# Summing the first adaLN half on the tensor engine, block by block, with x moved up among the first loads

## The chip, the cores and the metric

The kernel runs on one core of a Trainium2 chip. The metric is the device time of one execution in microseconds (us), the median of several runs. A core has a tensor engine (PE; its weight loads are shown apart as PEld), a vector engine (DVE), a scalar engine (ACT), GpSimd (POOL) and a sync engine (SP), which here issues the large loads. Each engine takes its instructions in a fixed order and waits at the first that isn't ready.

## The reference, cut to what matters

The model is a decoder trunk of two layers over 256 rows of width 1024. Ahead of each sub-layer the rows are normalized, then scaled and shifted by vectors that come from a conditioning vector c through a large matrix, w_ada:

```
c_act = jax.nn.silu(c)
for layer in range(DEPTH):
    mod = jnp.einsum('bd,dn->bn', c_act, w_ada[layer]) + b_ada[layer]
    sh1, sc1, gt1, sh2, sc2, gt2 = [m[:, None, :] for m in jnp.split(mod, 6, axis=-1)]
    ...
    h = rms_norm(x, g_attn[layer]) * (1.0 + sc1) + sh1
    y = hybrid_mixer(h, ...)
    x = x + gt1 * y
    ...
```

The change is to how sh1 and sc1 of layer 0 are summed, for the first 512 of the 1024 columns. A "half" below is such a set: 512 columns of the shift and the same 512 of the scale, 1024 columns of w_ada together. A "block" is 128 of the 1024 rows of w_ada for one half, a tile of 128 x 1024 float32 (512 KB). Eight blocks make a half.

## The kernel before, in words

All is written in `trunk`. Everything is laid out for 128 partitions; the 256 rows of x are two tiles t of 128 rows, the width 1024 is eight chunks k of 128. Matrix products of activations with weights are made of three products of parts (`split_w` makes the two parts of a weight tile on ACT and DVE, `split_act` those of an activation).

The start stands between lines 407 and 472, in a pool of its own and under two rules. `in_order()` chains all DVE instructions of the block in the order in which they are written, and all ACT instructions likewise. PE's and SP's orders are left to the framework, which sorts by program order and by what is ready. Loads of w_ada in the start use eight buffers (`rada`, `bufs=8`); the ninth block can be loaded once the first buffer has been read.

The order as written:

- `first` and `second` are `Start` objects for half 0 and half 1. `block(k)` issues the load of block k on SP and then, on DVE, multiplies it with column k of the activated c (`cT`, one number for each partition) and adds it to `acc`, 128 x 1024 (lines 429 to 435).
- The first loop (line 438) goes over the eight blocks of half 0. Behind blocks 1 and 5 it issues the load of a tile of x, with its sum of squares (`nm0.part`, ACT) and its normalization (`nm0.finish`, ACT, with a small DVE and a small POOL step). At block 5 it also transposes the vectors (`vrows`) on PE; DVE copies out the norm's gains gT and the biases bT.
- `pj_i.split(0, 4)` loads and splits the first unit of w_in (line 451). Then comes block 0 of half 1.
- `first.sums()` (line 420) brings half 0 onto the partitions: `acc` still holds 128 partial sums per column. One matmul with the identity opens the accumulation in PSUM with the bias; eight matmuls, with 128 columns of `acc` each as the stationary operand and one column of ones as the moving one, sum over the partitions. The result `pc` has eight columns, four of shift and four of scale. `m1.take` (line 237) copies the shift and makes the gain on DVE.
- `modulated` (line 294) transposes four chunks of the normalized x on PE and applies gain and shift, for t = 0 on ACT and for t = 1 on DVE. `split_h` makes the two parts of h. Between these stand blocks 1 and 2 of half 1 on DVE.
- PE then runs the first half of the first projection (`pj_i.unit`, 324 columns) and most of the second (`pj_a.unit`, 512 columns), while DVE works off blocks 3 to 7 of half 1. `second.sums()` and its modulation follow, and with the second half of h the projections are finished. Attention begins behind that.

Of the kernel before, what the change touches and what calls it, by code (L numbers as in the profile page):

```python
# [12 lines left out]
F32 = mybir.dt.float32  # L13
# [7 lines left out]
P = 128  # L21
# [34 lines left out]
def trunk(ctx: ExitStack, tc: tile.TileContext, x, c, positions, w_in, w_out, diff_lambda, diff_subln,  # L56
          w_ada, b_ada, g_attn, g_ffn, w_ff_gate, w_ff_up, w_ff_down, w_router,
          w_exp_gate, w_exp_up, w_exp_down, g_final, out):
    nc = tc.nc
    V, A, T, G = nc.vector, nc.scalar, nc.tensor, nc.gpsimd  # L60
# [9 lines left out]
    def ps_b(name):  # L70
        return psum.tile([P, 512], F32, tag="b", name=name, bufs=2)

    def ps_c(name):
        return psum.tile([P, 512], F32, tag="c", name=name, bufs=2)
# [8 lines left out]
    def pre1(shape, dt, name):  # L83
        return pre.tile(shape, dt, name=name, bufs=1)
# [13 lines left out]
    ident = cst.tile([P, P], F32, name="ident")  # L98
# [9 lines left out]
    cT = pre1([P, KC], F32, "cT")  # L108
# [26 lines left out]
    @contextmanager  # L135
    def in_order(engines=(V.engine, A.engine)):

        ins = nc.cur_bb.bb.instructions
        n0 = len(ins)
        yield  # L140
        last = {}
        for i in ins[n0:]:
            if i.engine in engines:
                if i.engine in last:
                    tc.add_manual_dep(i, last[i.engine], mybir.DependencyInfo(
                        mybir.DependencyClass.NoSync, mybir.DependencyReason.DATA), reason="in_order")
                last[i.engine] = i.name
# [65 lines left out]
    class Mod:  # L213


        def __init__(self, l, which, g0, queue):
            self.l, self.base, self.g0, self.queue = l, which * 3072, g0, queue
            self.piece = 3 * which
            self.sh = cst.tile([P, KC], F32, name=f"sh{l}{which}")
            self.gain = cst.tile([P, KC], F32, name=f"gain{l}{which}")  # L220
# [41 lines left out]
    m1 = Mod(0, 0, 0, nc.scalar)  # L262
# [31 lines left out]
    def modulated(xn, mod, t, q, on_act):  # L294

        pt = ps_c("pt").rearrange("p (k s) -> p k s", k=4)
        hp = wk.tile([P, 4, P], F32, tag="hp", name="hp")
        for j in range(4):
            k = 4 * q + j
            T.transpose(pt[:, j], xn[:, t, k * P:(k + 1) * P], ident)  # L300
        for j in range(4):
            modulate(on_act, hp[:, j], pt[:, j], mod, 4 * q + j)
        return hp

    def split_h(hp, t, q, h1, h2):
        ks, s = slice(4 * q, 4 * q + 4), slice(t * P, (t + 1) * P)
        split_act(h1[:, ks, s], h2[:, ks, s], hp)
# [101 lines left out]
    with tc.tile_pool(name="start", bufs=1, reuse_waits="tile") as sp, tc.issue_after(silu_c.ins), in_order():  # L409

        bT = sp.tile([P, 2, KC], F32, name="bT")

        class Start:


            def __init__(self, q):
                self.q = q
                self.acc = pre.tile([P, 1024], F32, tag="ada", name="ada", bufs=ADAB)

            def sums(self):  # L420
                q = self.q
                pc = ps_b("pc")
                T.matmul(pc[:, 0:8].rearrange("p (a k) -> p a k", a=2), ident, bT[:, :, 4 * q:4 * q + 4],
                         start=True, stop=False)
                for j in range(8):
                    T.matmul(pc[:, j:j + 1], self.acc[:, j * P:(j + 1) * P], ones[:, 0:1], start=False, stop=j == 7)
                m1.take(q, pc)

            def block(self, k):
                r = sp.tile([P, 1024], F32, tag="rada", name="rada", bufs=8)  # L430
                nc.sync.dma_start(r, w_ada[0, self.q, k])
                if k == 0:
                    V.tensor_scalar(self.acc, r, cT[:, 0:1], None, op0=ALU.mult)
                else:
                    V.scalar_tensor_tensor(self.acc, r, cT[:, k:k + 1], self.acc, op0=ALU.mult, op1=ALU.add)

        first, second = Start(0), Start(1)
        for k in range(KC):
            first.block(k)
            if k in (1, 5):  # L440
                t = k // 5
                nc.sync.dma_start(xs[:, t], x[0, t * P:(t + 1) * P, :])
                for n in range(2):
                    nm0.part(t, n)
                nm0.finish(t, True)
            if k == 5:
                pv = ps_c("pv")
                T.transpose(pv[:, 0:48], vrows, ident[:48, :48])
                V.tensor_copy(gT, pv[:, 0:32])
                V.tensor_copy(bT.rearrange("p a k -> p (a k)"), pv[:, 32:48])  # L450
        vi = pj_i.split(0, 4)
        second.block(0)
        first.sums()
        hps = [modulated(nm0.xn, m1, t, 0, t == 0) for t in range(NT)]
        for t in range(NT):
            second.block(1 + t)
            split_h(hps[t], t, 0, *h)
        pj_i.unit(0, 4, vi)
        *va, a2 = pj_a.split(0, 4, True)
        pj_a.unit(0, 4, va, terms=(0, 1))  # L460
        for k in range(3, KC):
            second.block(k)
        a2()
        *vi, i2 = pj_i.split(4, 4, True)
        second.sums()
        hps = [modulated(nm0.xn, m1, t, 1, t == 1) for t in range(NT)]
        for t in range(NT):
            split_h(hps[t], t, 1, *h)
            if t == 0:
                i2()  # L470
        pj_i.unit(4, 4, vi)
        pj_a.unit(0, 4, va, terms=(2,))
# [468 lines left out]
    with tc.tile_pool(name="ffn", bufs=1, reuse_waits="tile") as fp:  # L941
# [5 lines left out]
        m1 = Mod(1, 0, 8, nc.gpsimd)  # L947
# [585 lines left out]
```

## Time and profile before

| | us |
|---|---|
| median of 3 runs | 1309.76 (1303.88 to 1314.73) |
| profiled execution, its own time | 1308.91 |
| its span, first to last instruction | 1307.1 |
| PE busy | 1230.5 (94%) |
| DVE busy | 1091.4 (83%) |
| ACT busy | 832.9 (64%) |
| DMA | 396.90 MB, mean 304 GB/s |

The times in the rows below count from the first instruction. "Busy" of PE includes matmuls that stand in the pipeline behind one another, so a full PE is not PE at its peak. The granted clock (PEclk) is the share of the full TensorE clock of 2.4 GHz that the hardware granted; the record of it begins with its first change.

### The profile page before, as it was taken

The numbers are of one execution on the slowest core, as the hardware profiler recorded it, in microseconds if no ns is written. First come the engines' busy times: TensorE is split into PE (matmuls) and PEld (weight loads), VectorE is DVE, ScalarE is ACT, GpSimd is POOL, SyncE is SP. The second block draws the span as 40 slices with busy tenths as digits, with TensorE's granted clock in tenths as the row PEclk, the third lists the DMA queues.
The fourth block names the chain that finished last, engine by engine and source line by source line (L and its number), as shares of the span: only waits on it lengthen the run. The fifth ranks groups of instructions, "written<-read, shape, count | busy, mean of one in ns | idle before, by whom it ended". The sixth has DMA issues, their size and how long they took to land.

```text
span 1307.1 us, 17866 instructions
## 1 busy us (share of the span) xinstructions
PE 1230.5 (94%) x6601; PEld 1036.0 (79%) x6601; DVE 1091.4 (83%) x1236; ACT 832.9 (64%) x1010; POOL 52.5 (4%) x88
## 2 busy tenths in 40 slices
PE   4989899999999899899999999999999999999996
PEld 4779779989887787677888877788878778788784
DVE  7898677787768864687899987899986999978996
ACT  3654563433446555457788856788855898667785
POOL 3101000010001000000000000000000000000001
PEclk9999899999989899889999999999999999999999
DMA  9557828988963433568999998899998999998991
GB/s 382 206 170 239 293 93 309 318 315 302 331 241 113 137 122 129 225 235 290 385 396 420 419 412 308 324 404 420 421 382 292 358 419 420 420 350 319 410 361 56
DMA packets 63679, 396.90 MB, mean 304 GB/s; under 512 B 7718, under 2 KB 8032, under 8 KB 23264
## 3 DMA queue, kind: packets, MB, share of 16 engines
q1 hardware_dynamic: 62928, 395.60, 79.4%
q8 instruction: 54, 0.88, 0.3%
q14 instruction: 41, 0.34, 0.1%
q0 software_dynamic: 640, 0.07, 0.0%
q10 hardware_dynamic: 16, 0.00, 0.0%
HBM read 394.60 MB, written 1.05 MB: 303 GB/s over the span
## 4 chain that ended last, share of the span: by engine, by line
PE 62%; DVE 10%; issue 8%; ACT 4%; POOL 0%; POOLq 0%; ACTq 0%; DVEq 0%
DVE w L168 6%; PE gu L187 5%; PE gu L186 5%; PE gu L188 5%; PE gu L1269 4%; PE gu L1268 4%; PE dn L186 4%; PE dn L188 4%; PE dn L187 4%; PE pj L340 3%; PE dn L1268 3%; PE dn L1269 2%; PE ptl L1284 2%; PE gu L870 2%; PE gu L872 2%
## 5 line engine op out<-in xcount | busy, mean ns | idle before, releaser
L164 ACT ACTIVATE w<-raw 128x1024 fp32r<-128x1024 f32 (+3 forms) x203 | 258.9, 1293 | 164.4 <-PE gu L871 37.2
L168 DVE TENSOR_TENSOR w<-raw,w 128x1024 fp32r<-128x1024 f32 (+3 forms) x203 | 303.8, 1512 | 50.8 <-ACT w L164 50.3
L168 DVE TENSOR_TENSOR w<-rawx,w 128x2048 fp32r<-128x2048 f32 (+1 forms) x134 | 300.2, 2252 | 26.5 <-ACT w L164 26.2
L164 ACT ACTIVATE w<-rawx 128x2048 fp32r<-128x2048 f32 (+1 forms) x134 | 252.2, 1887 | 16.4 <-PE gu L187 9.2
L340 PE MATMUL pj<-w,h 128*128 128x384 f32 (+3 forms) x672 | 134.0, 351 | 1.2 <-ACT h L182 0.5
L211 DVE SCALAR_TENSOR_TENSOR ada<-rada,cT,ada 128x1024 f32<-128x1024 f32 x80 | 102.3, 1279 | 32.7 <-DMA rada<-in_w_ada 32.6
L340 PEld LDWEIGHTS pj<-w,h 128*128 128x128 f32 x672 | 112.9, 192 | 11.4 <-ACT h L182 2.4
L168 DVE TENSOR_TENSOR w2x<-rawx,w1x 128x2048 fp32r<-128x2048 f32 (+1 forms) x45 | 100.6, 2237 | 12.9 <-ACT w1x L164 12.9
L186 PE MATMUL gu<-w,hh 128*128 128x512 f32 (+1 forms) x288 | 110.5, 384 | 0.0
L1269 PE MATMUL gu<-w,hh 128*128 128x512 f32 (+1 forms) x288 | 107.4, 380 | 3.2 <-DVE w L168 2.8
L187 PE MATMUL gu<-w,hh 128*128 128x512 f32 (+1 forms) x288 | 109.2, 379 | 0.0
L188 PE MATMUL gu<-w,hh 128*128 128x512 f32 (+1 forms) x288 | 109.1, 379 | 0.0
L1268 PE MATMUL gu<-w,hh 128*128 128x512 f32 (+1 forms) x288 | 106.7, 377 | 0.0
L870 PE MATMUL gu<-h,w 128*128 128x256 f32 x320 | 91.5, 286 | 0.0
L872 PE MATMUL gu<-h,w 128*128 128x256 f32 x320 | 90.6, 283 | 0.0
L871 PE MATMUL gu<-h,w 128*128 128x256 f32 x320 | 90.5, 283 | 0.0
L164 ACT ACTIVATE w1x<-rawx 128x2048 fp32r<-128x2048 f32 (+1 forms) x45 | 84.4, 1878 | 4.7 <-PE gu L187 2.5
L1269 PEld LDWEIGHTS gu<-w,hh 128*128 128x128 f32 x288 | 54.1, 188 | 18.8 <-DVE w L168 8.5
L188 PEld LDWEIGHTS gu<-w,hh 128*128 128x128 f32 x288 | 54.6, 190 | 10.8
L187 PEld LDWEIGHTS gu<-w,hh 128*128 128x128 f32 x288 | 54.8, 190 | 10.4 <-issue 0.5
L186 PEld LDWEIGHTS gu<-w,hh 128*128 128x128 f32 x288 | 54.6, 190 | 10.5 <-issue 0.5
L1268 PEld LDWEIGHTS gu<-w,hh 128*128 128x128 f32 x288 | 54.1, 188 | 10.4
(348 smaller groups left out, 2508.7 us busy)
## 6 DMA issues: line engine op xcount, KB each, us to landing
rawx<-in_w_exp_down SPq DMA_DIRECT2D x72, 1024.0 KB, 7.4
rawx<-in_w_exp_up SPq DMA_DIRECT2D x55, 1024.0 KB, 7.6
rawx<-in_w_exp_gate SPq DMA_DIRECT2D x49, 1024.0 KB, 8.3
rada<-in_w_ada SPq DMA_DIRECT2D x96, 512.0 KB, 5.2
raw<-in_w_exp_gate SPq DMA_DIRECT2D x39, 1024.0 KB, 8.0
raw<-in_w_exp_up SPq DMA_DIRECT2D x33, 1024.0 KB, 7.8
raw<-in_w_exp_down SPq DMA_DIRECT2D x16, 1024.0 KB, 7.3
raw<-in_w_ff_gate SPq DMA_DIRECT2D x11, 1024.0 KB, 7.1
```

Of the source, the lines that this page charges most:

```text
L164: last_split[0] = A.activation(v1[:, s], r[:, s], AF.Copy)
L168: last_split[1] = V.tensor_tensor(v2[:, s], r[:, s], v1[:, s].bitcast(F32), op=ALU.subtract)
L186: T.matmul(ps, l1, r1, start=start, stop=False)
L187: T.matmul(ps, l2, r1, start=False, stop=False)
L188: T.matmul(ps, l1, r2, start=False, stop=stop)
L211: V.scalar_tensor_tensor(acc, r, cT[:, k:k + 1], acc, op0=ALU.mult, op1=ALU.add)
L340: T.matmul(o, (h1, h2, h1)[i][:, k, s], (v1, v1, v2)[i][:, j], start=(k == 0 and i == 0), stop=(k == KC - 1 and i == 2))
L870: T.matmul(pg[:, b], v1[:, k, s], h[0][:, k], start=(k == 0), stop=False)
L871: T.matmul(pg[:, b], v1[:, k, s], h[1][:, k], start=False, stop=False)
L872: T.matmul(pg[:, b], v2[:, k, s], h[0][:, k], start=False, stop=(k == KC - 1))
L1268: T.matmul(ps, l1, r1, start=start, stop=False)
L1269: T.matmul(ps, l1, r2, start=False, stop=stop)
```

## The change

Half 0 gets no `acc` any more. A PSUM tile `pc` is opened with a matmul of the identity with a tile of zeros. For each block, as it lands, eight matmuls take 128 columns of the block as the stationary operand and column k of cT as the moving one, and add to the eight columns of `pc`: the product with c and the sum over rows are one step. The bias matmul now closes the accumulation, and `take` follows as before. The loads of x are issued behind blocks 0 and 2 instead of 1 and 5, the transposes of the vectors at block 4 instead of 5. Half 1 stays as it was.

```diff
-        first, second = Start(0), Start(1)
+        second = Start(1)
+
+        pc = ps_b("pc")
+        zero = sp.tile([P, 8], F32, name="zero")
+        V.memset(zero, 0.0)
+        T.matmul(pc[:, 0:8], ident, zero, start=True, stop=False)
         for k in range(KC):
-            first.block(k)
-            if k in (1, 5):
-                t = k // 5
+            r = sp.tile([P, 1024], F32, tag="rada", name="rada", bufs=8)
+            nc.sync.dma_start(r, w_ada[0, 0, k])
+            for j in range(8):
+                T.matmul(pc[:, j:j + 1], r[:, j * P:(j + 1) * P], cT[:, k:k + 1], start=False, stop=False)
+            if k in (0, 2):
+                t = k // 2
                 nc.sync.dma_start(xs[:, t], x[0, t * P:(t + 1) * P, :])
                 for n in range(2):
                     nm0.part(t, n)
                 nm0.finish(t, True)
-            if k == 5:
+            if k == 4:
                 pv = ps_c("pv")
...
         vi = pj_i.split(0, 4)
         second.block(0)
-        first.sums()
+        T.matmul(pc[:, 0:8].rearrange("p (a k) -> p a k", a=2), ident, bT[:, :, 0:4], start=False, stop=True)
+        m1.take(0, pc)
```

## Rows read from the trace of the kernel before

**Rows 1.** Windows of the start: stretch, its length, busy us (instructions) by engine, PEclk, DMA share, GB/s.

```profile
5.50:17.00 11.50, 1.69 (x6) 1.07 (x6) 10.73 (x33) 4.16 (x11) 2.84 (x2) 1.00 1.03 413
...
25.90:31.10 5.20, 5.20 (x21) 5.15 (x21) 5.14 (x6) 2.35 (x3) 0.74 (x2) 1.00 1.04 411
31.10:36.20 5.10, 5.10 (x27) 4.32 (x26) 5.01 (x5) 1.38 (x2) 1.10 (x1) 1.00 1.01 412
```

**Rows 2.** Timeline of DVE in the start: start, duration, line, operation, out<-in, count.

```profile
5.89 0.96 DVE L353 CAST posf<-posi 2x128 f32<-2x128 int32 x1 [4.80 <-DMA posi<-in_positions]
...
8.77 0.74 DVE L433 TENSOR_SCALAR ada<-rada,cT 128x1024 f32<-128x1024 f32 x1
9.55 1.29 DVE L435 SCALAR_TENSOR_TENSOR ada<-rada,cT,ada 128x1024 f32<-128x1024 f32 x1
...
17.07 2.60 DVE L435 SCALAR_TENSOR_TENSOR ada<-rada,cT,ada 128x1024 f32<-128x1024 f32 x2
...
23.34 0.16 DVE L239 COPY sh<-pc 128x4 f32<-128x4 f32 x1 [1.52 <-PE pc L426]
...
28.48 6.56 DVE L435 SCALAR_TENSOR_TENSOR ada<-rada,cT,ada 128x1024 f32<-128x1024 f32 x5
```

**Rows 3.** Timeline of PE in the start.

```profile
4.84 0.27 PE L107 MATMUL pcr<-ident,crow 8*128 8x8 f32 x1 [4.84 <-POOL ident masks.py:199]
...
17.21 1.02 PE L423 MATMUL pc<-bT,ident 128*128 128x8 f32 x4 [1.70 <-DVE bT L450]
18.85 1.12 PE L300 MATMUL pt<-ident,xn 128*128 128x128 f32 x4 [0.61 <-ACT xn L284]
19.76 3.54 PE L426 MATMUL pc<-ones,ada 128*128 128x1 f32 x16
...
25.88 0.64 PE L340 MATMUL pj<-w,h 128*128 128x324 f32 x1
...
36.34 1.84 PE L426 MATMUL pc<-ones,ada 128*128 128x1 f32 x16
```

**Rows 4.** Line 426 from 19 to 24 us: durations in ns, min/median/max.

```profile
L426 PE MATMUL pc<-ones,ada x16: 340/352/352, 19.8 to 22.9; 128*128 128x1 f32 x16
```

**Rows 5.** SP's first and later w_ada issues, and each one's time to landing.

```profile
0.82 0.87 SPq L431 DMA_DIRECT2D rada<-in_w_ada  x2
DMA to landing us min/median/max: 3.5/3.5/3.5
...
4.73 1.27 SPq L431 DMA_DIRECT2D rada<-in_w_ada  x2
DMA to landing us min/median/max: 10.0/10.2/10.3
```

**Rows 6.** Windows of the projections' matmuls alone (tile pj).

```profile
26.00:31.10 5.10, 4.94 (x16) 4.38 (x17) 0.00 (x0) 0.00 (x0) 1.00 1.03 410
31.10:32.30 1.20, 1.20 (x10) 1.20 (x9) 0.00 (x0) 0.00 (x0) 1.00 1.05 432
```

**Rows 7.** Windows later on, around very narrow matmuls; columns as in rows 1.

```profile
360.90:362.20 1.30, 1.30 (x13) 1.30 (x13) 1.30 (x2) 0.28 (x1) 0.00 (x0) 1.00 0.98 403
363.20:369.00 5.80, 5.80 (x28) 5.80 (x29) 4.83 (x6) 3.18 (x4) 0.00 (x0) 0.50 0.73 238
...
543.20:546.50 3.30, 3.30 (x18) 3.17 (x17) 1.73 (x5) 2.13 (x6) 0.00 (x0) 0.50 0.68 281
546.60:549.90 3.30, 3.30 (x17) 3.08 (x17) 2.20 (x16) 2.11 (x5) 1.16 (x6) 0.50 0.01 2
550.00:553.00 3.00, 2.87 (x22) 2.25 (x22) 1.91 (x6) 2.49 (x3) 0.00 (x0) 1.00 0.00 0
```

**Rows 8.** Timeline of PE in those stretches.

```profile
360.86 2.28 PE L233 MATMUL pc<-ones,ada 128*128 128x1 f32 x16 [2.21 <-issue]
...
544.03 1.71 PE L984 MATMUL pl<-wr,hp 128*128 128x8 f32 x8
...
547.52 4.40 PE L1380 MATMUL pth<-ident,h 128*128 128x128 f32 x21
```

## The prediction

> **What bounds the kernel now.** I read the table of windows over the first 38 us first, then the timelines of PE and DVE there, then the landing of the loads, and last the granted clock wherever PE runs very narrow matmuls. In the windows the reader is to see a start that is full of DMA (its share stays above 1.0 from 5.5 to 36.2 us) while PE is nearly empty: 1.69 us busy in the 11.5 us to 17.0, against 10.73 for DVE [rows 1]. DVE spends that time on the first half's sum over w_ada: the first block's multiply of 0.74 us at 8.77, then seven multiply-adds, the last pair from 17.07 to 19.67 [rows 2]. PE then turns the sum into columns in 16 records from 19.76 to 23.30, and DVE picks the result up at 23.34 [rows 2, 3]. I call that moment T0.
>
> From T0 everything up to 38 us hangs on one thread. DVE's fixed order goes on with the seven remaining blocks of the second half, the last five from 28.48 to 35.04, 11.7 us behind T0 [rows 2]. PE starts the projection at 25.88 and is full to 36.2 [rows 1, 3]; the second half's columns start at 36.34, 13.0 us behind T0 [rows 3]. Behind this come the second half of h, the first projection's end, and attention. PE is 94% busy over the span, so I see nothing further on that would take up a shift of T0, and count it one for one.
>
> **The change part by part.** *Removed:* 0.74 + 7 x 1.29, some 9.8 us of DVE [rows 2], and the 16 records after the sum, 3.54 us [rows 3]. Both lay on the path to T0, so all of it comes free; the question is what stands there instead.
>
> *Added on PE:* for each of eight blocks 8 calls, 64 in all. A call of this form (fp32, 128x128 weights, one moving column) leaves two weight loads and two matmuls: the 8 calls of the old sum are the 16 records [rows 3]. So the change issues 128 records instead of 16. The pace of the old ones is the price: 16 took 3.54 us, one by itself lasts 0.35 [rows 4], so the spacing is (3.54 - 0.35) / 15 = 0.213 us. The same 16 at 36.34 took 1.84, about half [rows 3]. So one block costs 3.4 us at the slow pace or 1.7 at the fast one, where a 512 KB block lands every 1.3 us: the first lands at 0.82 + 3.5 = 4.3, the last of the eight, issued about 5.7, at about 16.0 (nine loads later, 11.7 us) [rows 5]. At either pace PE is the limit and not the loads.
>
> Which pace? The page shows the granted clock as 1.00 from the start, but the rows contradict that: the projection's matmuls of 324 columns run 16 in 5.1 us before 31.1 and 10 in 1.2 us after it [rows 6], a step by two, which I read as 1.2 and then 2.4 GHz. PE had been full since 25.9 by then. What raises the clock is told by the places where the record does show it. From 543.2 to 546.5 PE was busy in 3.30 of 3.30 us, mostly with matmuls of 8 moving columns, and the granted clock stayed at 0.50; eight of those records took 1.71 us, 0.214 each. It stood at 0.50 through the transposes of 128 columns from 547.52 too, and was back at 1.00 from 550 [rows 7, 8]. From 360.9 the 1-column form itself ran: busy in 1.30 of 1.30 us at 1.00, after a pause; then the clock fell in the midst of these 16 records, which is why they took 2.28 us, and it stayed at 0.50 for 5.8 us of full wide matmuls [rows 7, 8]. So, as far as these rows go, a PE that is busy with one or eight columns does not gain the full clock, and does not hold it behind a pause. The new records are all of one column, and what runs among them is eight transposes. I therefore take 0.213 throughout; the other end is half of it.
>
> The Trainium skill, "TensorE: Matmul & The Clock Gate", section "What's actually happening", says the array is throttled by default and activity releases it; read as engine busy time, that would give the fast pace soon after the start, and it is the second rival below. The stretch at 543 us speaks against that reading. The same page, section "LDWEIGHTS (loading the stationary operand)", puts a load of 128 columns at 107 ns; by that price 128 loads are 13.7 us instead of 27.3, and the end would come out at 1308.8. The trace does not agree at the lower clock: 0.213 from load to load.
>
> *The sum to T0.* PE is free of the transpose of c at 4.84 + 0.27 = 5.1 [rows 3]. The zero matmul that opens the accumulation is two records like those of the bT matmul (four in 1.02 us, 0.255 each [rows 3]): 0.5. The blocks: 128 x 0.213 = 27.3. PE must also run the eight transposes of xn (four in 1.12 us [rows 3], so 2.2), the two small ones of positions and vectors (at most 0.28 each, 0.6), and both bT matmuls (four records, 1.0). Together 5.1 + 0.5 + 27.3 + 2.2 + 0.6 + 1.0 = 36.7, and 0.1 to the pickup: T0 = 36.8 instead of 23.3, later by 13.5 us. Nothing of it is hidden: DVE, in its written order, has only the first weight unit's subtraction and the second half's first multiply before it waits for T0.
>
> *Moved:* x is issued behind blocks 0 and 2 instead of 1 and 5, so the first half of x lands one load (1.3 us) earlier and the second three. I cost this at nothing: the rows normalized last were transposed from 18.85 [rows 3], before T0 as it is, and the new T0 is later still. The order of loads changes nothing in their number.
>
> *The new wait on SP:* the second half's blocks need the eight buffers of the first, and PE now frees these, the last about T0. Behind them in SP's order stand the later units of w_in. Block 15 then lands 3.5 to 10.3 us after issue [rows 5], 40.3 to 47.1; DVE wants it about 10.5 us after T0 (the last of the five from 28.48, 33.8 before), 47.3. So this wait is covered, by little at the worst end; if it isn't, a us or two is added.
>
> *After T0* the chain of 13.0 us is as it was: PE comes to the projection at the lower clock in both kernels.
>
> The profiled execution took 1308.9 us (span 1307.1 and 1.8 around it), 0.9 under the median of the three runs shown. 1308.9 + 13.5 = 1322.4.
>
> **The rivals.**
>
> *Late order.* The zero memset could stand on DVE behind the cast that waits for positions until 5.89 and lasts 0.96 [rows 2], or where DVE had its first block before, at 8.77; PE would start at 6.9 to 8.8. Or PE meets a transpose before its xn is there. That adds 1.8 to 5: 1324 to 1327. For it: DVE's order at that place was not by arrival before either (block 0 had landed at 4.3). An upper bound on the pitch itself is 0.35, a record with no overlap: 128 x 0.14 = 17.8 more, 1340; the same form ran at 0.213, so I give this next to nothing.
>
> *The clock rises while the blocks are summed.* Suppose it takes 5.2 us of a busy PE, as from 25.9 to 31.1. Then 24 records go at 0.213 to 10.8, 104 at 0.107 to 21.9, and the rest (3.8) at half, 1.9: T0 = 23.8, half a us late. The projection then starts at the full clock and saves 2.6 us of 5.2, so that DVE's 11.7 us behind T0 is the last instead of 13.0, 1.3 less. In sum 0.8 less: about 1308.1. For it: PE would be busy without a gap. Against it: the stretches at 363 and 543 us.
>
> *The other side: faster.* If the fast pace held from the first block (the page's 1.00), the 31.6 us of PE work would be 15.8: T0 = 21.0, 2.3 earlier, and with the 1.3 of the projection 3.6: 1305.3. It decides where the mean pitch falls under 18.2 / 31.6 x 0.213 = 0.123 us, at which T0 is 23.3 as before. Against it: the old sum's own 16 records, at the same place in the program, ran at 0.213.
>
> **How the numbers follow.** Forecast 0.72, late order 0.11, rising clock 0.11, fast from the start 0.05, something else 0.01. The forecast's own range is 1319 to 1325 (an order of PE without gaps and one with short ones, and when the clock rises in the projection). The range of 8 in 10 goes from 1308, which takes in the rising clock, to 1328, which takes in the late order. Over 1%, about what a measurement of this kernel tells from no change, is 13.1 us: the forecast's 13.5 stands on that line, so its 0.72 splits, 0.37 slower and 0.35 within. Late order is slower (0.11). Rising and fast clock lie within 1% (0.16, of which I give 0.02 to faster, for scatter). Slower 0.48, same 0.50, faster 0.02.
>
> **What the profile after would show.** Right: 128 records of the new line between 5 and 37 us, 16 in about 3.4 us, with PE full; no multiply-add on DVE before the second half; the copy of the shift at about 36.8 and the second one 15 us later; loads of w_ada that wait on PE; DMA share well under 1.0 between 18 and 36. Wrong, if the same 16 records speed up on the way, or if the first projection starts before 30 us. Then the step that failed is the pace at which one-column matmuls run, and with it the reading of the clock. If T0 is at 37 and the time is not 10 us longer, the step that failed is that nothing behind it takes up the shift.

## The result, and the profile after

| | before | after |
|---|---|---|
| median, us (6 runs each) | 1310.88 | 1326.62 |
| ratio, 95% interval | | 1.013 (1.0099 to 1.0161) |
| span of the profiled execution, us | 1307.1 | 1321.5 |
| T0, the copy of the first half's shift | 23.34 | 38.56 |
| the same copy for the second half | 38.23 | 52.55 |

The kernel became slower by 1.0 to 1.6%. The profiled execution after is longer by 14.4 us; T0 came 15.2 us later and the second half's copy 14.3 us. So in these two executions the whole loss is there before the first projection is finished. DVE in the kernel after from T0 on, and the second copy of the kernel before (start, duration, line, operation, out<-in, count, and in brackets the wait before it):

```profile
38.56 0.16 DVE L239 COPY sh<-pc 128x4 f32<-128x4 f32 x1 [17.66 <-PE pc L461]
...
43.70 6.56 DVE L435 SCALAR_TENSOR_TENSOR ada<-rada,cT,ada 128x1024 f32<-128x1024 f32 x5
...
52.55 0.16 DVE L239 COPY sh<-pc 128x4 f32<-128x4 f32 x1
```

```profile
38.23 0.16 DVE L239 COPY sh<-pc 128x4 f32<-128x4 f32 x1 [0.91 <-PE pc L426]
```

All kernels named in the rows below are read from their own profiled execution.

PE in the start of the kernel after, in order of time (start, duration, line, out<-in, count):

```profile
6.92 0.26 PE L355 MATMUL pp<-ident,posf 2*128 2x2 f32 x1 [1.80 <-DVE posf L353]
7.12 0.60 PE L442 MATMUL pc<-zero,ident 128*128 128x8 f32 x2
8.57 0.31 PE L456 MATMUL pv<-ident,vrows 48*128 48x48 f32 x1 [0.85 <-DVE ang L374]
8.81 17.22 PE L447 MATMUL pc<-cT,rada 128*128 128x1 f32 x80
25.89 0.88 PE L300 MATMUL pt<-ident,xn 128*128 128x128 f32 x3
26.57 3.41 PE L447 MATMUL pc<-cT,rada 128*128 128x1 f32 x16
...
34.67 3.41 PE L447 MATMUL pc<-cT,rada 128*128 128x1 f32 x16
37.95 0.57 PE L461 MATMUL pc<-bT,ident 128*128 128x8 f32 x2
...
42.52 8.09 PE L340 MATMUL pj<-w,h 128*128 128x324 f32 x38
...
50.67 1.84 PE L426 MATMUL pc<-ones,ada 128*128 128x1 f32 x16
```

This answers [rows 3]: in place of 16 records from 19.76 to 23.30 there are 128, from 8.81 to 38.1, with the eight transposes of xn among them. Sixteen of them, one block, take 3.41 us. The same in sum, by line, from 5 to 39 us (count, busy us, mean ns of one, idle before):

```profile
L447 PEld LDWEIGHTS pc<-cT,rada 128*128 128x128 f32 x128 | 27.7, 333 | 0.1
L447 PE MATMUL pc<-cT,rada 128*128 128x1 f32 x128 | 27.6, 350 | 0.0
```

The weight loads are full for 27.7 us with 0.1 us of idle time: between these records PE waits for nothing, and the loads of w_ada land sooner than PE can take them. The windows of the kernel after, columns as in [rows 1] (the 1.00 under PEclk is no measurement here, since it stands ahead of the first recorded change of the clock), and its longest waits in the first 56 us (who waited for whom, us in total, times, longest):

```profile
5.50:17.00 11.50, 9.22 (x43) 9.05 (x43) 4.32 (x27) 5.19 (x12) 4.36 (x6) 1.00 1.02 412
17.00:38.00 21.00, 21.00 (x102) 21.00 (x101) 2.24 (x3) 1.38 (x2) 0.00 (x0) 1.00 0.64 226
```

```profile
ACT hp L290 <- DVE gain L240: 27.8, 2, 19.6
POOL kTI L530 <- PE pc L461: 22.2, 1, 22.2
DVE sh L239 <- PE pc L461: 17.7, 1, 17.7
```

From 17 to 38 us PE is busy in 21.00 of 21.00 us, DVE in 2.24 and ACT in 1.38, and the DMA share, 1.01 to 1.04 in the rows of the kernel before [rows 1], is 0.64. DVE waits 17.7 us for the sum in one piece, and ACT 19.6 for the gain. The engines have changed places: DVE was the full one, now it is PE, and PE needs longer.

### The profile page after: what moved, and what is told of

Read it like the earlier page. It is cut to its first block, busy times and chain, and to the rows that moved or that the text cites. A ratio compares the mean times of both kernels' runs of the same rounds, so it can differ in the third digit from the quotient of the medians.

```text
span 1321.5 us, 18081 instructions
## 1 busy us (share of the span) xinstructions
PE 1254.2 (95%) x6715; PEld 1059.9 (80%) x6715; DVE 1082.4 (82%) x1229; ACT 832.7 (63%) x1010; POOL 50.5 (4%) x88
## 3 DMA queue, kind: packets, MB, share of 16 engines
HBM read 394.60 MB, written 1.05 MB: 299 GB/s over the span
## 4 chain that ended last, share of the span: by engine, by line
PE 59%; DVE 12%; issue 9%; ACT 4%; POOL 0%; POOLq 0%; DVEq 0%; ACTq 0%
DVE w L168 7%; PE gu L187 5%; PE gu L186 5%; PE gu L188 5%; PE dn L186 4%; PE dn L188 4%; PE dn L187 4%; PE gu L1278 3%; PE gu L1277 3%; PE pj L340 3%; PE gu L879 2%; PE gu L881 2%; PE gu L880 2%; ACT w L164 2%; PE dn L1277 2%
```

## The experiments

Ratios are to the kernel before, run on the same chip in the same session. In the first session its median was 1306.06 us, in the second 1307.29, in the third 1307.61. Results of the kernels' wide matmuls that are told of below are thrown away; nothing of the computation is left out.

### The moved part alone

```diff
-            if k in (1, 5):
-                t = k // 5
+            if k in (0, 2):
+                t = k // 2
...
-            if k == 5:
+            if k == 4:
```

> The kernel before with only the moved part of the change: x issued behind blocks 0 and 2, the vectors transposed at block 4, the sum still on DVE. Theory (the whole loss comes from the tensor engine's 128 narrow records): the moved part is worth nothing, T0 (the copy of the shift) stays at 23.3 within 1 us, the time within 2 us of before. Rival (the moved loads themselves cost, because the blocks land later): T0 later by one or two loads, 1.3 to 2.6 us, and the time by as much.

Measured: 1307.53 us, ratio 1.0004 (0.9972 to 1.0036). T0 at 23.91, second copy at 37.80. The moved part alone changes the time by no more than 0.4% either way, so the loss belongs to the sum. (T0 is 0.6 us later. The trace shows no wait of DVE in that stretch: its multiply-adds start at 10.93 instead of 9.55, behind small steps that stood among the blocks before, and the last one ends at 20.2 instead of 19.7. Which of the steps costs this was not tested.)

### Another order on PE

Line numbers apart, the kernel after, with the rope tables (and with them the positions' transpose) moved behind block 4, and PE's transpose of the vectors ordered behind that block:

```diff
+    def tables():
         posf = pre1([NT, P], F32, "posf")
...
             if k == 4:
-                pv = ps_c("pv")
-                T.transpose(pv[:, 0:48], vrows, ident[:48, :48])
+                with tc.issue_after(mm.ins):
+                    pv = ps_c("pv")
+                    T.transpose(pv[:, 0:48], vrows, ident[:48, :48])
...
+                    tables()
```

> The kernel after with another order on the tensor engine: the rope tables and the transpose of the vectors stand behind block 4, so the blocks can start once c is activated. Theory (of the 15.2 us by which T0 came later, 3.2 are the wait of the first block behind the positions and the vectors, the rest is 128 records at 0.213): first block at 5.6 instead of 8.8, T0 at 35.3, the time 3 us under the kernel after. Rival (the loss is the pace alone and the early records wait for loads instead): first block earlier, but T0 at 37 or later and the time less than 1.5 us under after.

Measured: 1320.32 us, ratio 1.0094 (1.0063 to 1.0126). PE in its start:

```profile
5.05 0.59 PE L446 MATMUL pc<-zero,ident 128*128 128x8 f32 x2
5.50 17.20 PE L451 MATMUL pc<-cT,rada 128*128 128x1 f32 x80
...
32.10 3.41 PE L451 MATMUL pc<-cT,rada 128*128 128x1 f32 x16
35.37 0.57 PE L467 MATMUL pc<-bT,ident 128*128 128x8 f32 x2
```

The first block starts at 5.50 instead of 8.81, T0 comes at 35.99 instead of 38.56 (2.6 earlier), the second copy at 50.21 instead of 52.55 (2.3). The ratio is 0.0036 lower than that of the kernel after, 4.7 us, but the two were measured in different sessions and their intervals overlap (1.0099 to 1.0126), so the times alone don't tell them apart; the traces do. Some 2.5 us of the loss are PE's order: the first block stood behind two transposes that waited for late inputs. Of the 3.3 us by which it came earlier 2.6 are left at T0, less than expected. The other 12.7 us to T0 remain with the blocks started right behind the activation of c; they are PE's work at this pace.

### 64 moving columns instead of one

The zero tile and the matmul that opens `pc` grow to 512 columns with it.

```diff
-                T.matmul(pc[:, j:j + 1], r[:, j * P:(j + 1) * P], cT[:, k:k + 1], start=False, stop=False)
+                T.matmul(pj64[:, j], r[:, j * P:(j + 1) * P], cT[:, k:k + 1].to_broadcast([P, 64]), start=False, stop=False)
```

> The kernel after with one size changed: each of the 64 calls has 64 moving columns (column k of c repeated) instead of 1, the same weight loads, the same number of records. Theory (the tensor engine stays at 1.2 GHz because its matmuls are of one column): with 64 columns the same records speed up from 0.213 to about 0.11 to 0.12 us on the way, T0 at about 27 us, the first projection at the full clock from its start, and the time 9 to 13 us under the kernel after. Rival 1 (busy time decides, and the one-column stream was slow for another reason, such as waiting for loads or two weight loads a call): the pace stays at 0.213, T0 at 38 to 39, the time as after. Rival 2 (wider is dearer): pace over 0.213, slower than after.

Measured: 1323.97 us, ratio 1.011 (1.0038 to 1.0182). The theory fell, in the form that it had:

```profile
8.97 17.17 PE L448 MATMUL pc<-cT,rada 128*128 128x64 f32 x80
26.07 0.34 PE L457 MATMUL pv<-ident,vrows 48*128 48x48 f32 x1
26.34 10.50 PE L448 MATMUL pc<-cT,rada 128*128 128x64 f32 x48
```

80 records in 17.17 us are 0.215 each, as with one column (17.22), and the last 48 are no faster than the first. T0 is 37.21, earlier than in the kernel after because PE ran the eight transposes of xn behind the blocks and not among them. Two things follow. The columns are free at this size: 64 cost what one costs, so the pace is that of the weight loads, or of a fixed cost for each load and matmul; the runs don't part these two. And it isn't the single column that keeps the pace low; a stream of fp32 weight loads with 64 columns each stays at it just as well, through 28 us of a full PE.

### Wide matmuls ahead of the blocks, and among them

Whether 0.213 us is the clock at all was still open: it could have been the path of the weights. 24 matmuls of 512 bf16 columns were put between the zero matmul and the first block:

```diff
+        wb = sp.tile([P, 512], BF16, name="wb")
+        V.memset(wb, 0.5)
...
+                    after = T.matmul(pj_a.ps[0], wb[:, :P], wb, start=True, stop=True).ins
...
+            with tc.issue_after(last):
                 for j in range(8):
```

and in the second kernel, besides, a pair of them ahead of every second call within the blocks (8 for 16 records).

> The kernel after, with 24 wide matmuls (bf16, 512 columns, their result is thrown away) between the zero matmul and the first block; the blocks stay as they are, one column a call. With 64 columns a call the pace did not change (0.214 us), so the theory now reads: a stream that consists mostly of fp32 weight loads does not count as activity, with 1 or 64 columns, and only wide matmuls raise the clock. Theory: the burst of some 8 to 10 us raises the granted clock near its end; the first blocks then run at about 0.11 us a record and fall back to 0.213 some us later; T0 at about 41 to 44. Rival (a busy engine holds a clock that it has): all 128 records at 0.11, T0 at 29 to 32. Second rival (0.213 is not the clock but the path of the weights from freshly landed tiles): 0.213 from the first record on although the granted clock shows 1.00.

> The same burst, and 8 of the wide matmuls within each block besides, one pair ahead of every second call. Theory (wide matmuls among them keep the clock): the granted clock rises and stays at 1.00 to the end of the blocks, 16 records and 8 wide matmuls take about 3.5 us a block at that clock, T0 at 42 to 45. Rival (the narrow stream pulls the clock down even so): 6.8 us a block, T0 at 65 or later.

Measured, one run each: 1322.82 and 1327.14 us; T0 39.75 and 40.33, both earlier than expected, since the burst took 6.84 us and not 8 to 10. Windows of the records of `pc` alone (busy of PE, PEld, DVE, then PEclk, DMA share, GB/s), first with the burst alone, then with wide matmuls among them:

```profile
14.30:17.40 3.10, 3.10 (x30) 3.10 (x29) 0.00 (x0) 1.00 1.06 381
17.50:20.60 3.10, 3.10 (x17) 3.10 (x16) 0.00 (x0) 0.50 0.71 213
20.60:23.70 3.10, 3.10 (x16) 3.10 (x16) 0.00 (x0) 0.50 0.61 168
```

```profile
14.80:17.90 3.10, 1.95 (x16) 2.35 (x16) 0.00 (x0) 1.00 1.06 433
...
35.00:38.10 3.10, 1.93 (x17) 2.33 (x18) 0.00 (x0) 1.00 0.97 338
```

With the burst alone the same loads run at 29 in 3.1 us (0.107 each) while the granted clock is 1.00, and at 16 in 3.1 us (0.194 by this count, 3.41 us for 16 later) once it is 0.50. The fall comes between 17.4 and 17.5 us, 3.2 us into the narrow stream, with PE busy in every one of those windows: being busy in the profile's sense did not hold the clock that PE had. With wide matmuls among the records the clock stays at 1.00 to the end, and four records take 0.50 us throughout. So the pace is the clock, and what kept it up here were the wide matmuls. As a remedy it is worth nothing: the wide ones cost PE the time that the clock saves, T0 is no earlier.

### Two blocks on PE, six on DVE

PE opens the accumulation and takes blocks 0 and 1 directly while it is idle (NPE is 2); DVE sums the other six, and the 16 records add their sum. First with x at blocks 0 and 2, then with x at 1 and 5 as in the kernel before:

```diff
-            first.block(k)
+            if k < NPE:
+                first.direct(k)
+            else:
+                first.block(k, k == NPE)
```

> A mixture: the tensor engine takes blocks 0 and 1 directly (32 records, 6.8 us, while it is idle anyway), DVE sums blocks 2 to 7 as before, x early as in the kernel after. Theory (the direct sum costs only what does not fit into the idle time of the tensor engine): the direct records end by 16, DVE ends 1.3 us behind the landing of block 7, at 17.3 to 18.5, the 16 records follow at the slow pace, T0 at 21 to 22 and the time 1 to 2.5 us under the kernel before. Rival (the tensor engine's narrow work delays the transposes or the bias ahead of the sum): T0 at 23.3 or later and the time not under before.

> The mixture of two blocks on the tensor engine and six on DVE, now with x at blocks 1 and 5 as in the kernel before. In the mixture with x early DVE sat idle for 2.5 us behind the first of its blocks, because the step that follows x in its written order waited for ACT. Theory: without that wait DVE ends its blocks at 17.1 to 17.5, T0 at 21 and the second copy of the shift some 2 us earlier than before, the time 1.5 to 2.5 us under the kernel before. Rival (what follows T0 is held by the second half's loads or by the projection at the lower clock): T0 at 21 but the second copy at 37.5 or later, no gain.

Measured: with x early 1306.62 us, ratio 1.0000 (0.9965 to 1.0035), T0 at 24.04; with x as before 1305.79 us, ratio 0.9985 (0.9965 to 1.0005), T0 at 21.59, second copy at 35.84. DVE with x early, then with x as before:

```profile
10.41 0.74 DVE L454 TENSOR_SCALAR ada<-rada,cT 128x1024 f32<-128x1024 f32 x1
13.63 0.21 DVE L278 TENSOR_SCALAR var<-ss 128x1 f32<-128x1 f32 x1 [2.48 <-ACT xn L272]
...
16.45 3.92 DVE L456 SCALAR_TENSOR_TENSOR ada<-rada,cT,ada 128x1024 f32<-128x1024 f32 x3
```

```profile
11.18 3.92 DVE L456 SCALAR_TENSOR_TENSOR ada<-rada,cT,ada 128x1024 f32<-128x1024 f32 x3
15.02 0.21 DVE L278 TENSOR_SCALAR var<-ss 128x1 f32<-128x1 f32 x1
...
15.32 2.60 DVE L456 SCALAR_TENSOR_TENSOR ada<-rada,cT,ada 128x1024 f32<-128x1024 f32 x2
```

With x early the step after x waits 2.48 us for ACT, with blocks 3 to 7 behind it in the written order, and that eats what two blocks less on DVE had gained; the forecast of T0 at 21 to 22 missed that. With x as before nothing waits, DVE ends at 17.9 instead of 19.7, and T0 and the second copy come 1.8 and 2.4 us earlier. The median is 1.5 us under that of before, within the interval of no change.

The same with four blocks on PE:

> The mixture with x at blocks 1 and 5, now with four blocks on the tensor engine and four on DVE. Theory (each further block costs the tensor engine 16 records at 0.213, 3.4 us, and what doesn't fit ahead of DVE's end is added to T0): the direct records end at about 22.2, transposes and bias follow, then the 16 records; T0 at 28 to 29.5, against 21.6 with two blocks. Rival (the loads or DVE set T0): T0 under 24.

Measured: T0 28.56, second copy 42.45; 1306.04 us in a single run, which tells nothing beside a scatter of several us.

```profile
8.95 13.81 PE L431 MATMUL pc<-cT,rada 128*128 128x1 f32 x64
...
25.11 3.41 PE L438 MATMUL pc<-ones,ada 128*128 128x1 f32 x16
```

Two more blocks put T0 7.0 us later, 3.5 each. For two blocks PE has the idle time; the two further ones were paid in full.

### Wide matmuls in the kernel before

The kernel before has 16 records of the same form and the first projection at the low clock. 26 wide matmuls behind the transpose of the vectors and 7 behind the records, then 36 and 8:

> The kernel before, with 26 wide matmuls whose result is thrown away on the idle tensor engine ahead of the 16 records, and 7 behind them. Theory (what limits the records and the first projection is the clock at 1.2 GHz): the granted clock is up before 19.7, the 16 records take 1.8 instead of 3.5 us, T0 at 21.6, the projection of 324 columns runs at the full clock from its start (saves 2.6 us), the second copy of the shift 3 us earlier than before, the time 2 to 4 us under the kernel before. Rival (the pauses around the records bring the clock down again): T0 at 21.6 to 23.3, the projection as slow as before, gain under 1.5 us. Second rival (the wide matmuls delay the transposes): T0 later than 23.3.

> As the kernel before with wide matmuls on the idle tensor engine, now 36 ahead of the 16 records instead of 26 and 8 behind them. With 26 the granted clock had risen at 11.9 us and fallen again at 18.8, in the pauses ahead of the records. Theory (without those pauses the clock holds): granted clock 1.00 from about 12 us on, the 16 records in 1.84 us, T0 at 21.6, the first projection at the full clock, the second copy of the shift at 34 to 35.5 instead of 38.2, the time 3 to 4 us under the kernel before. Rival (the clock falls all the same, or 36 wide matmuls are too late for the sum): T0 at 23.3 or later, second copy at 37 or later, gain under 2 us.

Measured: 1303.53 us, ratio 0.9973 (0.9951 to 0.9995), and 1305.47 us, ratio 0.9973 (0.9948 to 0.9998). T0 at 23.35 and 22.64, second copy at 37.53 and 36.53. The first in windows, columns as in [rows 1], the second as PE's timeline:

```profile
12.00:18.70 6.70, 5.03 (x27) 2.62 (x25) 6.59 (x13) 3.42 (x6) 1.73 (x2) 1.00 1.02 412
18.80:23.00 4.20, 4.14 (x20) 3.98 (x21) 3.03 (x4) 1.28 (x3) 0.00 (x0) 0.50 1.03 417
```

```profile
8.99 10.71 PE L445 MATMUL pj<-wb 128*128 128x512 bf16 x36
...
20.76 1.84 PE L426 MATMUL pc<-ones,ada 128*128 128x1 f32 x16
...
34.40 1.95 PE L426 MATMUL pc<-ones,ada 128*128 128x1 f32 x16 [1.02 <-DVE ada L436]
```

With 26 the clock was up (from about 12 us on a wide matmul's record lasts 0.38 us, before that 0.63) and fell before the records came, behind pauses of PE; T0 did not move. With 36 it held: the 16 records take 1.84 us instead of 3.54. But by the same sign the clock rose only at about 15 us here, not at 12 as expected, so the last wide matmul ends at 19.7 with eight transposes still to come. The records start 1.1 us after DVE has ended, and T0 gains 0.7. The projection then runs at the full clock, and PE idles 1.02 us for DVE: behind T0 the limit is now DVE's order, 11.8 us from T0 to the end of its last block. The 2.7 to 4.2 us expected at the second copy became 1.7.

These two are under the kernel before by 0.3% with intervals that end just below 1. In the first of the two the start accounts for 0.7 us of a median 3.8 lower; the rest of that I can't assign.

### How the start passes through

| kernel | T0 | second copy | span | span less second copy |
|---|---|---|---|---|
| before | 23.34 | 38.23 | 1307.1 | 1268.9 |
| after | 38.56 | 52.55 | 1321.5 | 1269.0 |
| x moved alone | 23.91 | 37.80 | 1307.5 | 1269.7 |
| other order | 35.99 | 50.21 | 1316.3 | 1266.1 |
| 64 columns | 37.21 | 52.63 | 1323.6 | 1271.0 |
| two blocks, x as before | 21.59 | 35.84 | 1301.2 | 1265.4 |
| two blocks, x early | 24.04 | 37.93 | 1299.9 | 1262.0 |
| four blocks | 28.56 | 42.45 | 1304.3 | 1261.9 |
| 26 wide ahead | 23.35 | 37.53 | 1296.1 | 1258.6 |
| 36 wide ahead | 22.64 | 36.53 | 1304.6 | 1268.1 |
| burst, then the blocks | 39.75 | 55.26 | 1321.0 | 1265.7 |
| wide among the blocks | 40.33 | 56.24 | 1325.4 | 1269.2 |

These are single profiled executions. What follows the second copy takes 1258.6 to 1271.0 us; it scatters by several us, more than the small edits move, but it is not shorter where the start is late (1265.7 to 1271.0 in the five kernels with the second copy behind 50 us). So none of these traces shows the delay taken up behind the start; a part of it as small as the scatter could not be seen.

## Why the prediction came out as it did

The forecast was 1322.4 us, slower by 13.5; measured was a ratio of 1.0099 to 1.0161, which on the profiled 1308.9 is 13.0 to 21.1 us, and 14.4 between the two profiled executions. Direction and cause were as forecast. The median after, 1326.62, lies above the forecast's own range of 1319 to 1325, inside the wider one, and in the 1324 to 1327 of the rival called late order, which is also what the trace shows. Part of that distance is the base: the six runs of the kernel before have their median 2 us above the 1308.9 that the sum starts from. By its steps:

- *Removed.* Right: DVE's blocks and the 16 records are gone, and DVE has 2.24 us of work in the 21 us to 38.
- *128 records at 0.213, 27.3 us.* Right: 128, 27.7 us busy, 3.41 for a block, and PE rather than the loads the limit.
- *When PE starts.* This term was mis-sized. The sum let PE go on at 5.1, with the zero matmul, and booked the two small transposes as 0.6 us of work. They were waits: PE's order has the positions' transpose at 6.92, behind an input that is late, and the vectors' at 8.57, and the first block at 8.81 instead of 5.6. That is the rival called late order, with another culprit than the one named (the zero memset ran at 1.05). Undoing it was worth 2.6 us at T0. By the sum the first block was due at 6.2 with those two counted, so 2.6 late; the eight transposes and the bT matmuls, priced at 3.2 with each group's last drain in it, took 0.9 less. Hence T0 at 38.56 instead of the forecast 36.8.
- *After T0, 13.0 us as before.* It was 12.1 to the second half's records (50.67), since the clock rose sooner in the projection: its 38 matmuls took 8.09 us instead of 8.99. This took 0.9 us back, and with the term above the forecast of the shift, 13.5, comes to 14.3 at the second copy. That the two are so close is in part luck. The start was missed by 2.6 us, and two smaller misses of 0.9 went the other way, the second of them by chance: the same 38 matmuls took 7.99 us in the kernel with x moved alone and 8.98 in that with the burst.
- *The wait of SP on PE, at nothing.* It is there: SP waited 22.6 us in seven waits for PE to free buffers. It was covered, as forecast; DVE's last five blocks run without a gap from 43.70.

```profile
SPq L431 <- PE pc L447: 22.6, 7, 3.8
```

- *x earlier, at nothing.* Right for the time (1.0004), though with DVE on the path it costs 0.6 us at T0, which the forecast did not see.
- *What raises the clock.* The conclusion held, that the records stay at the lower clock; the reason given for it was too narrow. The rows [rows 7, 8] were read as "one or eight columns". 64 columns did no better. The burst and the mixed stream show what the rows of before could not: a PE that is full of such records loses a clock that it had been granted, and wide matmuls among them keep it. The rival of the rising clock is thereby excluded here, by 28 us of full PE in two kernels without a rise.

The Trainium skill, "TensorE: Matmul & The Clock Gate", section "What's actually happening", says that activity releases the throttle. These runs agree only where activity is not taken for the busy time of the profile: the granted clock fell to 0.50 with PE busy in 3.10 of 3.10 us on either side of the fall. The rule of its section "LDWEIGHTS (loading the stationary operand)", which for 128 columns comes to 107 ns, agrees with the loads at the full clock, 0.107 us from one to the next; at the lower one each took twice that.

Still open: what it is in a stream that keeps the clock. The runs show one stream on each side of it, fp32 weight loads with up to 64 columns and the same loads with wide matmuls among them, and nothing in between was tried. Wide matmuls are not the only work ahead of a rise: in the kernel before, the clock was back by 550 us with PE on transposes of 128 columns since 547.52 [rows 7, 8].

## What to carry to other kernels

Before a sum is moved from DVE to PE, count the weight loads and not the multiplications: 128 x 128 weights for one column were two loads in fp32, here 0.43 us a call at the low clock, and eight blocks of 512 KB cost 27 us where DVE took 10 and the loads landed in 12. Give an idle engine what fits into its idle time (here two blocks, 1.8 us at T0, though no gain clear of noise in the time) and leave the rest where it was. And in an engine's order look for what waits, not for what is long: two transposes of 0.3 us each held the first block for 3 us.

## What was not expected of the hardware

- 64 moving columns cost the same as one beside fp32 weight loads: 80 records in 17.17 and 17.22 us.
- A TensorE at 1.00 of its clock fell to 0.50 in the midst of a stream in which it was busy without a gap (29 loads in 3.1 us before the fall, 16 after it).
